# Value products of a head pair as one scheduling unit in two attention stages

## The chip, the cores and the metric

The kernel runs as one program on one core of a Trainium2 chip. The metric is the device time of one launch in microseconds (us), median of the runs shown. Lower is better. Engines are named as the profile names them: PE is TensorE (PEld its weight loads), DVE is VectorE, ACT is ScalarE, POOL is GpSimd, SP is the engine that issues the DMAs here.

## The reference

Two blocks of two layers each follow one another on 512 tokens of width 1024. Layer 0 is a gated pooling mixer, layer 1 stick-breaking attention, layer 2 latent attention (MLA) with a context of 256 tokens, layer 3 differential attention; each is followed by a residual step. The two stages that matter here, cut down:

```python
# stick-breaking attention, 16 heads of 64, strictly causal
A[t,s] = beta[t,s] * prod_{s<j<t} (1 - beta[t,j])      # beta = sigmoid(q.k / sqrt(d))
o = einsum('bhts,bhsd->bhtd', A, v)

# latent attention, 16 heads, values of width 64, 512 tokens and 256 context tokens
p   = softmax(q @ [k, k_c].T * scale);   o   = p @ [v, v_c]
p_c = softmax(q_c @ k_c.T * scale);      o_c = p_c @ v_c
```

## The kernel before

The code is written in Python that records instructions into a tile framework. The framework's scheduler decides in what order each engine's instructions stand: it takes them by readiness and priority in a simulated time, and puts the semaphore waits in. The order of the source is thus a wish, not the order on the engine. Every engine then runs its own list strictly in order.

Both attention stages work by `pipeline`: a list of steps, each with a `first` part (logits on PE, then the elementwise work on ACT, DVE and POOL) and a `second` part, called some steps later, which turns the probabilities (`transpose`, line 172, into a PSUM tile `aT_p` or `PT_p`, then a copy to SBUF). Between the steps stand "pieces": projections that fill PE (`z_p`, `kb_p`, `vb_p`, `qb_p`) and the `ada` products (line 768), whose operands `araw` come by DMA from HBM.

When a pair of heads is finished, the products of probabilities and values are made:

- In the stick-breaking stage (414 to 547 us), once for each of 8 pairs: line 726, 8 matmuls into the PSUM tile `pv` (`pv1` in the source), for 4 key blocks j and the two heads e of the pair. Head 0 writes partitions 0 to 63 and head 1 partitions 64 to 127, so each matmul uses 64 columns of the array (128*64 in the profile).
- In the latent stage (780 to 1057 us), twice for each of 8 pairs: line 1057, 12 matmuls of 512 tokens for `PT` and 4 of 256 context tokens for `PTc`, again 128*64, with the two heads in turn.

A profile shows two MATMUL records for each of these fp32 matmuls, so that "x4" is two matmuls, one of each head, and "x2" a single one. The result is multiplied by the gate on DVE (lines 728 and 1058).

Weights come through `wraw`, three buffers of 512 KB that `araw` shares (lines 116 and 765): SP issues a DMA as soon as a buffer is free, ACT rounds it (line 126), POOL takes the rest (line 127).

Of the kernel before, what the change touches and what calls it, by code (L numbers as in the profile page):

```python
# [19 lines left out]
P = 128  # L20
# [3 lines left out]
NT = S // P  # L24
# [17 lines left out]
class Block:  # L42
# [601 lines left out]
    def stick_steps(self, c, ks, qs, vtok, ogs, pool):  # L644


        nc = self.nc
        h = {}
        half = (slice(0, 64), slice(64, 128))
        f = lambda ap: ap.bitcast(F32)  # L650

        def prep():

            Q = h["Q"] = [pool.tile([P, 512], F32R, tag=f"Q{e}", name="Q1", bufs=2) for e in range(2)]
            QL = h["QL"] = [pool.tile([P, 512], F32R, tag=f"QL{e}", name="QL1", bufs=2) for e in range(2)]
            K = h["K"] = [pool.tile([P, 512], F32R, tag=f"K{e}", name="K1", bufs=2) for e in range(2)]
            cs = slice((c % 2) * P, (c % 2 + 1) * P)
            pr = self.p_tr("kT_p")
            for t in range(NT):
                self.transpose(pr[:, t * P:(t + 1) * P], ks[c // 2][:, t, cs])  # L660
            for e in range(2):
                s, o = half[e], half[1 - e]
                nc.scalar.copy(K[e][s], pr[s])
                nc.vector.tensor_tensor(out=K[e][o], in0=pr[s], in1=f(K[e][s]), op=ALU.subtract)
            pr = self.p_tr("qT_p")
            for t in range(NT):
                self.transpose(pr[:, t * P:(t + 1) * P], qs[c // 2][:, t, cs])
            for e in range(2):
                s, o = half[e], half[1 - e]
                nc.scalar.activation(Q[e][s], pr[s], AF.Copy, scale=self.gqk[s])  # L670
                nc.scalar.activation(Q[e][o], pr[s], AF.Copy, scale=self.gqk[s])
                nc.vector.scalar_tensor_tensor(out=QL[e][s], in0=pr[s], scalar=self.gqk[s], in1=f(Q[e][s]), op0=ALU.mult, op1=ALU.subtract)
                nc.scalar.copy(QL[e][o], f(QL[e][s]))
            h["aT"] = [pool.tile([P, 13, P], F32, tag="aT", name="aT", bufs=4) for e in range(2)]

        def first(n, segs):
            if n == 0 and c == 0:
                prep()
            Q, QL, K = h["Q"], h["QL"], h["K"]
            L = self.p_lg("sb_l")  # L680
            for e, i, o in segs:
                w = (i + 1) * P
                qi = slice(i * P, (i + 1) * P)
                nc.tensor.matmul(L[:, o:o + w], lhsT=Q[e][:, qi], rhs=K[e][:, :w], start=True, stop=False)
                nc.tensor.matmul(L[:, o:o + w], lhsT=QL[e][:, qi], rhs=K[e][:, :w], start=False, stop=False)
                nc.tensor.matmul(L[:, o + i * P:o + w], lhsT=self.identb, rhs=self.maskb, start=False, stop=True)
            kp = pool.tile([P, 1024], F32, tag="sb_k", name="sb_k", bufs=2)
            bt = h["bt", n] = pool.tile([P, 1024], F32, tag="sb_b", name="sb_b", bufs=4)
            vw = (lambda t: t) if len(segs) == 3 else (lambda t: t.rearrange("p (a b) -> p a b", b=512)[:, :, :256])
            nc.scalar.activation(vw(kp), vw(L), AF.Sigmoid, scale=-1.0)  # L690
            nc.scalar.activation(vw(bt), vw(L), AF.Sigmoid)
            for e, i, o in segs:
                w = (i + 1) * P
                rev = slice(o + w - 1, o - 1 if o else None, -1)
                nc.vector.tensor_tensor_scan(out=kp[:, rev], data0=kp[:, rev], data1=kp[:, rev], initial=1.0, op0=ALU.mult, op1=ALU.min)  # L695

            for o, w in ((0, 1024),) if len(segs) == 3 else ((0, 256), (512, 256)):
                nc.gpsimd.tensor_tensor(out=bt[:, o:o + w - 1], in0=bt[:, o:o + w - 1], in1=kp[:, o + 1:o + w], op=ALU.mult)  # L698
            if n == 1 and "next" in h:
                h["next"]()  # L700

        def second(n, segs):
            aT, bt = h["aT"], h["bt", n]
            b0, pr = 0, None
            for e, i, o in segs:
                if b0 + i + 1 > 4:
                    b0, pr = 0, None
                if pr is None:
                    pr = self.p_tr("aT_p")
                for j in range(i + 1):  # L710
                    self.transpose(pr[:, (b0 + j) * P:(b0 + j + 1) * P], bt[:, o + j * P:o + (j + 1) * P])
                src = pr[:, b0 * P:(b0 + i + 1) * P].rearrange("p (j t) -> p j t", t=P)
                if i == 3:
                    nc.scalar.copy(aT[e][:, 3 * i:4 * i + 1, :], src)
                else:
                    nc.vector.tensor_copy(out=aT[e][:, 3 * i:4 * i + 1, :], in_=src)
                b0 += i + 1
            if n < 2:
                return
            self.need(c + 1)  # L720
            pv = self.p_pv("pv1")
            for j in range(NT):
                for e in range(2):
                    hd = 2 * c + e
                    av = aT[e][:, 4 * j:10 + j:3, :]
                    nc.tensor.matmul(pv[64 * e:64 * e + 64, j * P:], lhsT=vtok[j][:, hd * 64:(hd + 1) * 64], rhs=av, start=(j == 0), stop=(j == NT - 1))
            og = ogs[c // 2][:, (c % 2) * 512:(c % 2 + 1) * 512]
            nc.vector.tensor_tensor(out=og, in0=pv, in1=og, op=ALU.mult)

        if self.last_pair is not None:  # L730
            self.last_pair["next"] = prep
        self.last_pair = h
        tiles = [[(0, 3, 0), (0, 2, 512), (0, 0, 896)], [(1, 3, 0), (1, 2, 512), (1, 0, 896)], [(0, 1, 0), (1, 1, 512)]]
        return [(lambda n=n, t=t: first(n, t), lambda n=n, t=t: second(n, t)) for n, t in enumerate(tiles)]


# [261 lines left out]
    def mla_steps(self, h, grp, kTs, og, ogc, pool):  # L998
        nc = self.nc
        g, hh, e = h // 4, h % 4, h % 2  # L1000
        H = {}
# [39 lines left out]
        def second(qb):  # L1041
            for pe, dst, i in H[qb]:
                self.probs_T(pe, dst, i)
            if qb < 4:
                return
            if e == 0:
                return
            c = h // 2
            H0 = H["prev"]
            self.need(8 * g + 1)  # L1050
            V = grp["V", g]
            for nk, n, k0, px, o in ((6, 512, 0, "pt", og[c]), (2, 256, 4, "ptc", ogc[c])):
                pv = self.p_pv("pv2")[:, :n]
                for k in range(nk):
                    for ee, HH in ((0, H0), (1, H)):
                        vs = slice((hh - 1 + ee) * 64, (hh + ee) * 64)
                        nc.tensor.matmul(pv[64 * ee:64 * ee + 64, :], lhsT=V[:, k0 + k, vs], rhs=HH[px][:, k, :], start=(k == 0), stop=(k == nk - 1))  # L1057
                nc.vector.tensor_tensor(out=o, in0=pv, in1=o, op=ALU.mult)

        if self.chain:  # L1060
            self.chain[-1]["next"] = prep
            H["prev"] = self.chain[-1]
        self.chain.append(H)
        return [(lambda q=q: first(q), lambda q=q: second(q)) for q in range(5)]

    def soft(self, L, pool, W, bufs):
# [432 lines left out]
```

## Time and profile before

| what | value |
|---|---|
| median of 3 runs | 1595.64 us (1595.2 to 1601.13) |
| profiled execution, its own time | 1594.69 us |
| span of the profile | 1592.9 us |
| PE busy over the span | 1505.3 us (95%) |
| DVE, ACT, POOL busy | 58%, 46%, 38% |
| granted PE clock over the span, share of full | 0.983 |

The span is the time between the first and the last instruction of the profiled execution; 1.8 us of its time lie around it. A busy PE says that a matmul was in the array, not that it ran at its peak. [...]

### The profile page before, as it was taken

Reading aid. Unit: us, or ns where it says so; the run is one execution under the profiler, and the core shown is the slowest. Engines: PE = TensorE matmul, PEld = TensorE weight load, DVE = VectorE, ACT = ScalarE, POOL = GpSimd, SP = SyncE. Lnnn points to the kernel's source line nnn. Section 1 sums busy time; section 2 is a strip of 40 time slices with the busy share of each in tenths; the row PEclk is TensorE's granted clock in tenths of the full one; section 3 lists DMA queues with packets and bytes.
Section 4 is the critical chain, followed back from the end, with each engine's and each line's share of the span. In section 5 each row is a group of like instructions: output and inputs, shape, how many; then the busy total and the mean of one; then the engine's idle time right before and its main releaser. Section 6 shows DMA issues by size and latency. Waiting matters only on the chain.

```text
span 1592.9 us, 24439 instructions
## 1 busy us (share of the span) xinstructions
PE 1505.3 (95%) x9590; PEld 1253.3 (79%) x9590; DVE 927.9 (58%) x1769; ACT 733.8 (46%) x1347; POOL 603.4 (38%) x431
## 2 busy tenths in 40 slices
PE   6999999999899899999999999999798999999997
PEld 4777889997555678888876657579697999999987
DVE  6676465523766656442465566546866555556576
ACT  5323344436566433332565455543235554555642
POOL 2534555553444453212333222435442324343310
PEclk9999999999999999999999999999898999999999
DMA  5322432223244334311103030425421112111122
GB/s 157 105 79 89 123 118 83 98 84 115 81 132 133 106 120 124 87 44 50 50 1 120 5 120 2 145 80 186 132 69 55 41 41 67 40 56 52 54 74 100
DMA packets 149747, 136.01 MB, mean 85 GB/s; under 512 B 12612, under 2 KB 135224, under 8 KB 149632
## 3 DMA queue, kind: packets, MB, share of 16 engines
q1 hardware_dynamic: 149632, 134.45, 27.3%
q8 instruction: 76, 1.25, 0.3%
q14 instruction: 39, 0.32, 0.1%
HBM read 126.02 MB, written 8.40 MB: 84 GB/s over the span
## 4 chain that ended last, share of the span: by engine, by line
PE 41%; DVE 6%; ACT 5%; issue 3%; DMA 2%; POOL 1%; SPq 0%; DVEq 0%; POOLq 0%; ACTq 0%
PE PT_p L172 5%; PE pv L1057 4%; PE qkv_p L147 2%; PE qkv_p L149 2%; PE qkv_p L148 2%; PE pv L1420 2%; PE gt_p L147 2%; PE gt_p L148 2%; PE gt_p L149 2%; PE lg L147 2%; PE lg L148 2%; PE lg L149 2%; PE ada_p L768 1%; ACT pe L1074 1%; DMA wraw<-in_out_w_dram 1%
## 5 line engine op out<-in xcount | busy, mean ns | idle before, releaser
L127 POOL TENSOR_TENSOR wl<-wraw,wh 128x1024 fp32r<-128x1024 f32 (+2 forms) x159 | 376.4, 2376 | 379.5 <-ACT wh L126 366.3
L126 ACT CAST wh<-wraw 128x1024 fp32r<-128x1024 f32 (+2 forms) x164 | 166.4, 1020 | 281.2 <-issue 57.9
L1074 ACT ACTIVATE pe<-lg,st 128x768 f32<-128x768 f32 x160 | 130.5, 816 | 76.7 <-DVE st L1073 60.6
L1073 DVE TENSOR_REDUCE st<-lg 128x1 f32<-128x768 f32 x160 | 133.9, 845 | 38.4 <-PE lg L1401 20.1
L1036 POOL TENSOR_SCALAR pe<-pe,st 128x768 f32<-128x768 f32 (+1 forms) x96 | 73.6, 767 | 159.2 <-DVE st L1075 154.0
L147 PE MATMUL qkv_p<-wh,h 128*128 128x256 f32 x384 | 109.9, 286 | 0.8 <-ACT V L1346 0.7
L172 PEld LDWEIGHTS PT_p<-ident,pe 128*128 128x128 f32 x640 | 72.3, 142 | 47.8 <-issue 16.5
L149 PE MATMUL qkv_p<-wh,h 128*128 128x256 f32 x384 | 108.6, 283 | 0.2 <-DVE h L217 0.2
L148 PE MATMUL qkv_p<-wl,h 128*128 128x256 f32 x384 | 108.7, 283 | 0.0
L172 PE MATMUL PT_p<-ident,pe 128*128 128x128 f32 x640 | 99.9, 282 | 8.0 <-DVE pe L1406 3.0
L1405 POOL TENSOR_SCALAR pe<-pe,st 128x768 f32<-128x768 f32 x32 | 29.2, 912 | 126.2 <-DVE st L1404 80.3
L147 PE MATMUL out_p<-wh,o 128*128 128x256 f32 x256 | 74.7, 293 | 0.9 <-DVE y L1272 0.8
L147 PEld LDWEIGHTS qkv_p<-wh,h 128*128 128x128 f32 x384 | 73.1, 190 | 3.0 <-ACT V L1346 1.3
L148 PE MATMUL out_p<-wl,o 128*128 128x256 f32 x256 | 74.0, 291 | 1.3 <-POOL wl L127 1.3
L149 PE MATMUL out_p<-wh,o 128*128 128x256 f32 x256 | 73.7, 291 | 0.1
L149 PEld LDWEIGHTS qkv_p<-wh,h 128*128 128x128 f32 x384 | 73.0, 190 | 0.4 <-DVE h L217 0.4
L148 PEld LDWEIGHTS qkv_p<-wl,h 128*128 128x128 f32 x384 | 73.2, 191 | 0.0
L147 PE MATMUL kv_p<-wh,kv 128*128 128x256 f32 x256 | 72.1, 282 | 1.2 <-ACT kv L219 1.2
L148 PE MATMUL kv_p<-wl,kv 128*128 128x256 f32 x256 | 71.6, 280 | 0.0
L149 PE MATMUL kv_p<-wh,kv 128*128 128x256 f32 x256 | 71.1, 280 | 0.0
L698 POOL TENSOR_TENSOR sb_b<-sb_b,sb_k 128x1023 f32<-128x1023 f32 (+1 forms) x32 | 43.0, 1354 | 64.7 <-DVE sb_k L695 36.7
L695 DVE TENSOR_TENSOR_SCAN sb_k<-sb_k 128x512 f32<-128x512 f32 (+3 forms) x64 | 61.7, 1007 | 7.6 <-ACT sb_k L690 7.3
(456 smaller groups left out, 4568.1 us busy)
## 6 DMA issues: line engine op xcount, KB each, us to landing
araw<-in_ada_w_dram SPq DMA_DIRECT2D x48, 512.0 KB
wraw<-in_diff_w_in_dram SPq DMA_DIRECT2D x32, 512.0 KB
wraw<-in_out_w_dram SPq DMA_DIRECT2D x24, 512.0 KB
wraw<-in_a_w_in_dram SPq DMA_DIRECT2D x16, 512.0 KB
wraw<-in_ple_gate_w_dram SPq DMA_DIRECT2D x16, 512.0 KB
wraw<-in_w_kv_dram SPq DMA_DIRECT2D x16, 512.0 KB
wraw<-in_b_w_in_dram SPq DMA_DIRECT2D x16, 512.0 KB
wraw<-in_mla_w_in_dram SPq DMA_DIRECT2D x11, 512.0 KB
```

The costliest lines, as they stand in the source:

```text
L126: nc.scalar.copy(h[:, :n], raw[:, :n])
L127: (nc.vector if i < 3 or pool == "ow3" else nc.gpsimd).tensor_tensor(out=l[:, :n], in0=raw[:, :n], in1=h[:, :n].bitcast(F32), op=ALU.subtract)
L147: mm(out, lhsT=lh, rhs=rh, start=start, stop=False)
L148: mm(out, lhsT=lh, rhs=rl, start=False, stop=False)
L149: mm(out, lhsT=ll, rhs=rh, start=False, stop=stop)
L172: self.nc.tensor.transpose(out, in_, self.ident[:in_.shape[0], :in_.shape[0]])
L695: nc.vector.tensor_tensor_scan(out=kp[:, rev], data0=kp[:, rev], data1=kp[:, rev], initial=1.0, op0=ALU.mult, op1=ALU.min)
L698: nc.gpsimd.tensor_tensor(out=bt[:, o:o + w - 1], in0=bt[:, o:o + w - 1], in1=kp[:, o + 1:o + w], op=ALU.mult)
L1036: nc.gpsimd.tensor_scalar(out=pe, in0=pe, scalar1=st[:, 1:2], scalar2=0.0, op0=ALU.mult, op1=ALU.add)
L1057: nc.tensor.matmul(pv[64 * ee:64 * ee + 64, :], lhsT=V[:, k0 + k, vs], rhs=HH[px][:, k, :], start=(k == 0), stop=(k == nk - 1))
L1073: nc.vector.tensor_reduce(out=st[:, 0:1], in_=L, axis=AX.X, op=ALU.max, negate=True)
L1074: nc.scalar.activation(pe, L, AF.Exp, bias=st[:, 0:1], accum_out=st[:, 2:3])
```

## The change

The value products of a pair are put into a `tile_critical` section: one for each pair of the stick-breaking stage (8) and two for each pair of the latent stage (16), 24 in all. A section is one unit for the scheduler: nothing else is put between its instructions.

```diff
             pv = self.p_pv("pv1")
-            for j in range(NT):
-                for e in range(2):
-                    hd = 2 * c + e
-                    av = aT[e][:, 4 * j:10 + j:3, :]
-                    nc.tensor.matmul(pv[64 * e:64 * e + 64, j * P:], lhsT=vtok[j][:, hd * 64:(hd + 1) * 64], rhs=av, start=(j == 0), stop=(j == NT - 1))
+
+            with self.tc.tile_critical():
+                for j in range(NT):
+                    for e in range(2):
...
                 pv = self.p_pv("pv2")[:, :n]
-                for k in range(nk):
-                    for ee, HH in ((0, H0), (1, H)):
...
+
+                with self.tc.tile_critical():
+                    for k in range(nk):
+                        for ee, HH in ((0, H0), (1, H)):
...
```

The built program shows what a section becomes. Each is a block of instructions of its own on PE; all five engines leave their list by a branch there and go on in the next block. On PE two further instructions stand around it (NO_OP), and the branch into the section holds waits. The lines of the kernel move by 2 below the first section and by 4 below the second: line 726 becomes 728, line 1057 becomes 1061.

First place: PE at the first pair of the latent stage. `pv` is the result of the products, `lg` the logits of a later step, `kb_p` a projection, `PT_p` and `qT_p` turned tiles. Before:

```order
L147 MATMUL lg_7149<-kTs_5790,qT_6924 128x512
L172 MATMUL qT_p<-ident,qs 96x128 x4
L148 MATMUL lg_7149<-kTs_5790,qT_6924 128x512
L172 MATMUL qT_p<-ident,qs 96x128 x2
L1057 MATMUL pv_7129<-PT,V 64x512 x2
L147 MATMUL kb_p<-kvlat,wh 128x256
L148 MATMUL kb_p<-kvlat,wh 128x256
L149 MATMUL kb_p<-kvlat,wl 128x256
L1057 MATMUL pv_7129<-PT,V 64x512 x2
L172 MATMUL PT_p<-ident,pe 128x128 x4
L1057 MATMUL pv_7129<-PT,V 64x512 x7
L149 MATMUL lg_7149<-kTs_5790,qT_6924 128x512
```

One further matmul of this unit stands 69 rows earlier, by itself. In the changed program, with the waits of each row:

```order
L148 MATMUL lg_7169<-kTs_5806,qT_6940 128x512
L172 MATMUL qT_p<-ident,qs 96x128 [waits Activation_49]
L172 MATMUL qT_p<-ident,qs 96x128
L1057 NO_OP [waits PE_sequencer_49,DVE_49,Activation_49]
L149 MATMUL lg_7169<-kTs_5806,qT_6940 128x512
L1499 UNCONDITIONAL_BRANCH [waits DMAHW2_49,DMAHW1_49,DMAHW3_49,DMAHW0_49,DMAHW4_49,PE_sequencer_49,DMAHW5_49,DVE_49,DMAHW6_49,PE_49,DMAHW7_49,Activation_49,Pool_49]
L1061 MATMUL pv_7145<-PT,V 64x512 x12
L1057 UNCONDITIONAL_BRANCH
L147 MATMUL lg_7169<-kTs_5806,qT_6940 128x256 [waits PE_49]
L1057 NO_OP [waits PE_sequencer_49]
L148 MATMUL lg_7169<-kTs_5806,qT_6940 128x256
L149 MATMUL lg_7169<-kTs_5806,qT_6940 128x256
```

The 12 products now stand together, and the branch ahead of them waits for all eight DMA queues, for DVE, ACT and POOL, and for PE itself; the row behind them waits for PE again. The values waited for are those that each engine reaches at the end of its own list ahead of the branch, so that everything listed there has to be finished. The four products of `PTc` stood together before, too, and get a section and a branch of the same kind.

Second place: PE at the third pair of the stick-breaking stage; `ada_t` are four small products of an `ada` piece. Before:

```order
L685 MATMUL sb_l<-K_4059,QL_4057 128x384
L726 MATMUL pv_4099<-aT,vtok_1840 64x512 x2
L726 MATMUL pv_4099<-aT,vtok_1841 64x384 x2
L726 MATMUL pv_4099<-aT,vtok_1842 64x256 x2
L726 MATMUL pv_4099<-aT,vtok_1843 64x128 x2
L775 MATMUL ada_t<-asel,ada_row 128x4 x4
```

Changed:

```order
L685 MATMUL sb_l<-K_4063,QL_4061 128x384
L723 NO_OP [waits PE_sequencer_49,DVE_49,Activation_49]
L777 MATMUL ada_t<-asel,ada_row 128x4 [waits DVE_49,Activation_49]
L777 MATMUL ada_t<-asel,ada_row 128x4 x3
L172 MATMUL aT_p<-ident,sb_b 128x128 [waits PE_49,Pool_49]
L1499 UNCONDITIONAL_BRANCH [waits DMAHW2_49,DMAHW1_49,DMAHW3_49,DMAHW0_49,DMAHW4_49,PE_sequencer_49,DMAHW5_49,DVE_49,DMAHW6_49,PE_49,DMAHW7_49,Activation_49,Pool_49]
L728 MATMUL pv_4103<-aT,vtok_1840 64x512 x2
L728 MATMUL pv_4103<-aT,vtok_1841 64x384 x2
L728 MATMUL pv_4103<-aT,vtok_1842 64x256 x2
L728 MATMUL pv_4103<-aT,vtok_1843 64x128 x2
L723 UNCONDITIONAL_BRANCH
L172 MATMUL aT_p<-ident,sb_b 128x128 [waits PE_49]
```

The products stood together before as well; what is new is the branch and that `ada_t` now stands ahead of it.

Third place: the DMAs that SP issues around the third pair's branch in the changed program (a branch on SP marks the end of the list that PE waits for):

```order
L116 DMA wraw_4169<-in_b_w_in_dram 128x8x128
L767 DMA araw_4204<-in_ada_w_2_dram 128x1024
L767 DMA araw_4208<-in_ada_w_2_dram 128x1024
L116 DMA wraw_4349<-in_b_w_in_dram 128x8x128
L1499 UNCONDITIONAL_BRANCH
L767 DMA araw_4385<-in_ada_w_2_dram 128x1024
```

The weight load `wraw_4349` is the last DMA ahead of the branch; before there was no branch, and no PE instruction waited for it at this place. Outside the two stages the lists of PE are the same in both programs: the first 2276 and the last 3691 of 9112 matmuls and loads.

## Rows read from the trace of the kernel before

**Rows 1.** Stages: window, length; busy us of PE, PEld, DVE, ACT, POOL; clock; DMA.

```profile
414.00:547.00 133.00, 118.91 (x666) 76.31 (x664) 87.66 (x131) 73.49 (x107) 65.11 (x40) 0.96 0.34 107
780.00:1057.00 277.00, 272.74 (x1581) 179.87 (x1580) 168.33 (x412) 157.06 (x356) 92.15 (x114) 0.99 0.19 58
```

**Rows 2.** PE in order of time, first latent pair: start, duration, line.

```profile
787.66 1.07 PE L1057 MATMUL pv<-PT,V 128*64 128x512 f32 x2
...
803.22 1.08 PE L1057 MATMUL pv<-PT,V 128*64 128x512 f32 x4
...
806.38 3.65 PE L1057 MATMUL pv<-PT,V 128*64 128x512 f32 x14
809.95 0.50 PE L149 MATMUL lg<-kTs,qT 96*128 96x512 f32 x1
```

**Rows 3.** PE in order of time: two matmuls in a row of 512 columns.

```profile
790.22 0.40 PE L148 MATMUL lg<-kTs,qT 96*128 96x512 f32 x1
790.45 0.39 PE L149 MATMUL lg<-kTs,qT 96*128 96x512 f32 x1
```

**Rows 4.** All engines in time: a copy on ACT and PE, which waited for it.

```profile
412.00 0.57 ACT L714 COPY aT<-aT_p 128x512 f32<-128x512 f32 x1
...
412.65 0.19 PEld L684 LDWEIGHTS sb_l<-K,Q 128*128 128x128 f32 x1 [0.84 <-ACT aT L714]
412.65 0.50 PE L684 MATMUL sb_l<-K,Q 128*128 128x512 f32 x1
```

**Rows 5.** Start of the program on POOL, across the only branch into the kernel's block.

```profile
0.34 0.10 POOL L1487 MEMSET const-uint8-127<- 128x1 uint8 x1
0.73 0.20 POOL masks.py:197 MEMSET ident<- 128x128 f32 x1 [0.29 <-POOLq L1487]
```

**Rows 6.** The page's DMA queue of instruction loads: packets, MB, share of 16 engines.

```profile
q8 instruction: 76, 1.25, 0.3%
```

**Rows 7.** All engines in time at the first, third, fifth and eighth stick-breaking pair.

```profile
414.52 2.37 PE L726 MATMUL pv<-aT,vtok 128*64 128x512 f32 x16
...
416.88 1.04 ACT L126 CAST wh<-wraw 128x1024 fp32r<-128x1024 f32 x1 [0.53 <-DMA wraw<-in_b_w_in_dram]
...
460.69 2.37 PE L726 MATMUL pv<-aT,vtok 128*64 128x512 f32 x16
...
462.99 1.06 PE L775 MATMUL ada_t<-asel,ada_row 128*128 128x4 f32 x8
...
463.68 1.04 ACT L126 CAST wh<-wraw 128x1024 fp32r<-128x1024 f32 x1 [2.72 <-DMA wraw<-in_b_w_in_dram]
...
500.98 2.38 PE L726 MATMUL pv<-aT,vtok 128*64 128x512 f32 x16
...
504.14 1.04 ACT L126 CAST wh<-wraw 128x1024 fp32r<-128x1024 f32 x1 [2.89 <-DMA wraw<-in_b_w_out_dram]
...
543.68 2.96 PE L726 MATMUL pv<-aT,vtok 128*64 128x512 f32 x16
...
544.16 0.37 SPq L116 DMA_DIRECT2D wraw<-in_b_w_out_dram  x1
```

**Rows 8.** Two stretches of 1 us behind it, columns as in rows 1.

```profile
546.00:547.00 1.00, 1.00 (x7) 0.57 (x4) 0.26 (x1) 1.00 (x4) 0.00 (x0) 1.00 1.00 303
547.00:548.00 1.00, 0.80 (x3) 0.19 (x1) 1.00 (x3) 1.00 (x4) 0.00 (x0) 1.00 0.72 101
```

**Rows 9.** DVE in time at the first latent pair.

```profile
802.89 0.69 DVE L996 TENSOR_TENSOR kTs<-kb_p,kTs 64x512 fp32r<-64x512 f32 x1
```

**Rows 10.** The third latent pair: PE in time, and a stretch of 1 us.

```profile
875.77 1.94 PE L1057 MATMUL pv<-PT,V 128*64 128x512 f32 x8
...
876.00:877.00 1.00, 1.00 (x6) 0.29 (x4) 0.94 (x2) 1.00 (x2) 0.00 (x0) 1.00 0.43 168
```

**Rows 11.** The longest idle time of PE in the stick-breaking stage, and the clock behind it.

```profile
426.49 1.12 PE L172 MATMUL qT_p<-ident,qtok 128*128 128x128 f32 x4 [3.73 <-DVE aT L716]
...
425.00:430.00 5.00, 3.51 (x11) 2.93 (x12) 3.55 (x5) 1.97 (x4) 2.27 (x3) 0.53 0.21 81
```

More of the change, by code (lines that the diff above doesn't have):

```diff
@@ L721, in second @@
             pv = self.p_pv("pv1")
-            for j in range(NT):
-                for e in range(2):
-                    hd = 2 * c + e
-                    av = aT[e][:, 4 * j:10 + j:3, :]
-                    nc.tensor.matmul(pv[64 * e:64 * e + 64, j * P:], lhsT=vtok[j][:, hd * 64:(hd + 1) * 64], rhs=av, start=(j == 0), stop=(j == NT - 1))
+            with self.tc.tile_critical():
+                for j in range(NT):
+                    for e in range(2):
+                        hd = 2 * c + e
+                        av = aT[e][:, 4 * j:10 + j:3, :]
+                        nc.tensor.matmul(pv[64 * e:64 * e + 64, j * P:], lhsT=vtok[j][:, hd * 64:(hd + 1) * 64], rhs=av, start=(j == 0), stop=(j == NT - 1))
             og = ogs[c // 2][:, (c % 2) * 512:(c % 2 + 1) * 512]
@@ L1053, in second @@
                 pv = self.p_pv("pv2")[:, :n]
-                for k in range(nk):
-                    for ee, HH in ((0, H0), (1, H)):
-                        vs = slice((hh - 1 + ee) * 64, (hh + ee) * 64)
-                        nc.tensor.matmul(pv[64 * ee:64 * ee + 64, :], lhsT=V[:, k0 + k, vs], rhs=HH[px][:, k, :], start=(k == 0), stop=(k == nk - 1))
+                with self.tc.tile_critical():
+                    for k in range(nk):
+                        for ee, HH in ((0, H0), (1, H)):
+                            vs = slice((hh - 1 + ee) * 64, (hh + ee) * 64)
+                            nc.tensor.matmul(pv[64 * ee:64 * ee + 64, :], lhsT=V[:, k0 + k, vs], rhs=HH[px][:, k, :], start=(k == 0), stop=(k == nk - 1))
                 nc.vector.tensor_tensor(out=o, in0=pv, in1=o, op=ALU.mult)
```

## The prediction

> **What bounds the kernel now.** I began with the busy time of the engines in the two stages [rows 1]. PE is busy for 272.74 of 277.00 us in the latent stage and 118.91 of 133.00 in the stick-breaking stage; the next engine, DVE, has 168.33 and 87.66. PE is therefore the bound in both: what shortens or delays PE's list shows in the end nearly in full, while the other engines have room, about 100 us and 45 us. The 14.1 us that PE stands idle in the stick-breaking stage are the only place where a new wait of PE might cost nothing.
>
> Next I read PE's rows in order of time around one latent pair, for what the change can gain [rows 2]. The 12 products of `PT` appear as x2 at 787.66 (one matmul by itself, 1.07 us), x4 at 803.22 (1.08 us), and the first seven matmuls of the x14 at 806.38 (3.65 us); another single one lies between the first two. A single matmul thus takes as long as two matmuls, one of each head. The two heads use 64 columns each, and side by side they run at the same time. One step in a chain of such pairs takes 1.94 - 1.08 = 0.86 us [rows 2, 10].
>
> Last I looked, at the pairs themselves, for what else is under way when the products start, since that is what the new branch will wait for [rows 7, 9, 10].
>
> **The gain.** Of a `PT` group of 12, two matmuls now run alone. By rows: 2 x 1.07 for the singles, 1.08 for the x4, and about 3.65 for the last seven, 6.87 in all. Grouped it is five steps of 0.86 and a last one of 1.08, 5.37. The 1.5 us that this gives back are less by two or three overlaps: a matmul that follows another one starts 0.23 us after it but takes 0.40 [rows 3], and most of such an overlap was there with the neighbours already. I take 1.3 us for each pair, 8 x 1.3 = **10.4 us** (10 to 12). The four `PTc` products and at least five of the eight stick-breaking groups stood together before, as the third pair does (2.37 us, x16) [rows 7], so 16 sections can gain nothing or next to nothing; what the other stick-breaking groups may gain I leave in the range.
>
> **The price of a bare section.** Every section empties PE before it and again behind it, since PE waits for itself at both places. I work one such edge out in three parts:
> - the lost overlap: 0.40 us for a matmul less the 0.23 us at which the next would have started, 0.17 [rows 3];
> - the semaphore: ACT's copy ends at 412.00 + 0.57 = 412.57, and the PE weight load that waited for it starts at 412.65, 0.08 [rows 4];
> - the first matmul behind a stop takes 0.50 instead of 0.40, 0.10 [rows 3, 4].
>
> Together 0.35, and two of them 0.70. Then there are two jumps of PE's list. No row shows a jump of PE in the stages. The nearest is at the start of the program, where POOL's MEMSET ends at 0.44 and the next starts at 0.73 behind the branch into the kernel's block, 0.29 [rows 5]; part of that may be the end of a write. The bounds are 0 and 0.29 for each jump. I take 0.10, since a jump to the instruction that stands next in memory has less to do than the start of a program. That makes 0.70 + 0.20 = 0.90 us a section, and 24 x 0.90 = **21.6 us**. The low bound has no cost of a jump and half of each edge (a weight load can run beside the wait): 24 x 0.35 = 8. The high bound is 24 x (0.70 + 0.58) = 31.
>
> **What the branch waits for beyond PE itself.** It waits for everything that stands in any engine's list ahead of it, all eight DMA queues too. In the stick-breaking stage this is mostly a weight load of 512 KB that SP gave out shortly before, and that no PE instruction needed yet:
> - First pair: the products started at 414.52; the DMA that ACT's cast waited for was there at 416.88 [rows 7]. That is 2.36, less about 1.06 us of PE work that now stands ahead, 1.3.
> - Third: 463.68 against 460.69, 3.0, less 0.9, because `ada_t` (462.99, 1.06 us long) and a turned block now stand ahead of the branch and fill PE: 2.1.
> - Fifth: 504.14 against 500.98, 3.2, less the same 0.9: 2.3.
> - Eighth: the load is given out at 544.16 [rows 7]. The DMA engines are full up to 547.00 and at 0.72 in the next microsecond [rows 8], so I put the landing at 547.3, 3.6 us behind the start of the products at 543.68.
>
> The sum is **9.3 us**. If SP gives these loads out so much earlier that they are half done, 3 are left; if the other four pairs meet one as well, it is 17. Queued behind the branch on PE are the products and the logits of the next step, on which ACT and DVE wait; so a wait here is not made up elsewhere.
>
> In the latent stage the DMAs are rarer (share 0.19 against 0.34 [rows 1]). At the third pair DMA is still at 0.43 in the microsecond up to 877.00, and the products started at 875.77: 1.2 [rows 10]. Otherwise the branch waits for DVE or ACT to end what they have in hand. At the first pair DVE's L996 ends at 802.89 + 0.69 = 803.58, and PE could have gone on at 803.22 + 0.23 (the spacing in [rows 3]) = 803.45: 0.13 [rows 2, 9]. 15 times that is 2.0, together **3.2 us**. Low bound 1 (only the third pair); high bound 16, if each section meets a whole further operation of DVE's 0.69 us [rows 9] and the DMAs of the third pair come again.
>
> [...]
>
> **What is absorbed.** PE's idle 14.1 us in the stick-breaking stage come from waits for DVE and ACT. While PE stands at a branch these catch up, so that the wait that follows is shorter. I take **-3** (0 to -8, about half of the idle time), since most of the new waits are for DMAs and lie elsewhere than the old ones.
>
> The branches of the other engines wait for nothing and lie in their free time; were that cover gone, they would cost 48 jumps of 0.10 each, 5 us. The lists of PE outside the two stages are the same, so I cost them at nothing.
>
> **Sum:** 1594.69 - 10.4 + 21.6 + 9.3 + 3.2 + 4 - 3 = 1619.4. The median of the runs is 0.95 above the profiled execution's own time; with that, 1620.
>
> [...]
>
> **The rivals.**
> - *Edges nearly free* (the other side). If the next weight loads and the sequencer's work run while PE empties, and if what the branch waits for is done by the time PE reaches it, a section costs some 0.3 us (one lost overlap of 0.17 and some semaphore). Then it is -10.4 + 24 x 0.3 + 2 = -1, and with a gain of 12 and 0.2 a section, -12 + 5 + 1 = -6: 1590 to 1595, still up to a microsecond lower if a stick-breaking group gains. For it speaks that PE's waits in the profile cost only 0.08 of semaphore; against it, that the DMAs in [rows 7] were not yet there. It decides below 10.4/24 = 0.43 us a section with no DMA waited for.
> - *A load of instructions at each jump.* The instruction queue moved 76 packets in 0.3% of 16 engines' span [rows 6], 0.003 x 16 x 1592.9 / 76 = 1.0 us each. With 48 jumps that is +48 in place of the 4.8: about 1663, and 1669 with the clock lowered more often. Against it: PE runs through 9112 matmuls and loads with no such stop to be seen, and the blocks follow each other.
> - *The engines that feed PE are stopped too.* In the latent stage ACT and DVE work ahead of PE. If PE now waits at all 16 branches for one whole operation of theirs, which PE would have met later at no cost, each costs some 0.69 more [rows 9]: +11, 1631.
> - *The change does nothing.* If the products stand together anyway, as 16 of the groups did, and the barriers fall into idle time, the time stays at 1595. The 4.3 us of idle time in the latent stage [rows 1] leave too little room for 16 sections; I count this with the first rival.
>
> **How the numbers follow.** A measurement of this kernel can tell about 0.5%, 8 us, from no change: 1587.7 to 1603.6 is "the same". The likely case has 0.55; its terms put it between 1600 and 1640. The edges that are nearly free have 0.23, of which a part lies under 1587.7, where stick-breaking gains would have to come on top: 0.08 faster. Stopped feeders have 0.14 and the loads of instructions 0.08. A range of 1598 to 1650 leaves out most of the first rival and the dearest one. Slower by over 0.5%: 0.55 + 0.14 + 0.08, 0.77; the same, 0.15.
>
> **What would show it.** Gain: the `PT` products as one row of x24 of some 5.4 us, no x2 by themselves. Edges: in the latent stage an idle time of PE ahead of each L1061 and behind it, together near 0.9 us; at 0.3 the first rival is right, at 2 the second, with more than a hundred packets in the instruction queue. Loads: at the first, third, fifth and eighth stick-breaking pair an idle time of 1 to 4 us that ends with a DMA. Clock: windows of 5 us behind those with less than 0.9. The prediction is wrong if both stages together grow by less than 8 us, or if the idle time sits elsewhere than at the 24 sections.

## The result

| kernel | median | runs |
|---|---|---|
| before | 1595.42 us (1593.05 to 1601.13) | 4 |
| changed | 1650.95 us (1647.45 to 1655.31) | 4 |

The changed kernel takes 1.0344 times as long (95% interval 1.0306 to 1.0381), 55.5 us more. The sign and the kind of cost were forecast; the size was not: 1620 was forecast, 24 us more, and the time lies just above the range, which ended at 1650.

### The profile page after: what moved, and what is told of

Same layout as the page of the kernel before. It is cut to its first block, busy times and chain, and to the rows that moved or that the text cites. A ratio compares the mean times of both kernels' runs of the same rounds, so it can differ in the third digit from the quotient of the medians.

```text
span 1648.0 us, 24761 instructions
## 1 busy us (share of the span) xinstructions
PE 1506.5 (91%) x9590; PEld 1255.4 (76%) x9590; DVE 919.4 (56%) x1769; ACT 733.3 (44%) x1347; POOL 600.7 (36%) x431
## 5 line engine op out<-in xcount | busy, mean ns | idle before, releaser
L127 POOL TENSOR_TENSOR wl<-wraw,wh 128x1024 fp32r<-128x1024 f32 (+2 forms) x159 | 376.4, 2376 | 394.5 <-ACT wh L126 372.4
L698 POOL TENSOR_TENSOR sb_b<-sb_b,sb_k 128x1023 f32<-128x1023 f32 (+1 forms) x32 | 42.5, 1337 | 84.2 <-DVE sb_k L695 60.9
L695 DVE TENSOR_TENSOR_SCAN sb_k<-sb_k 128x512 f32<-128x512 f32 (+3 forms) x64 | 57.2, 935 | 7.1 <-ACT sb_k L690 6.9
```

The lines of the kernel that those rows point to most:

```text
L127: (nc.vector if i < 3 or pool == "ow3" else nc.gpsimd).tensor_tensor(out=l[:, :n], in0=raw[:, :n], in1=h[:, :n].bitcast(F32), op=ALU.subtract)
```

## The profile after

The stages first, in the view of the stretches (window, length; busy us of PE, PEld, DVE, ACT, POOL; clock; DMA), the stick-breaking stage from the end of the logits ahead of the first pair to the first output product, and most of the latent stage:

```profile
414.92:578.46 163.54, 124.10 (x659) 75.71 (x659) 82.81 (x129) 71.35 (x103) 62.07 (x40) 0.87 0.28 87
815.00:1109.41 294.41, 264.17 (x1564) 177.67 (x1563) 163.20 (x407) 150.79 (x341) 90.97 (x113) 0.98 0.18 55
```

The same stretch of the stick-breaking stage was 132.05 us before, with 117.95 of PE busy (414.52 to 546.57). It is 31.5 longer: PE's idle time went from 14.1 to 39.4 us, +25.3, and its busy time rose by 6.2 at a granted clock of 0.87 of full speed against 0.96. Most of the loss is thus standing still; the slower products come on top.

To compare kernels I use the same four PE instructions in each trace: the start of the last `ada_p` ahead of the first pair (411.66 before, 411.99 changed), the first `o_p` (546.57, 578.46), the first `lat_ss` (698.30, 732.55) and the first `out_p` (1056.18, 1109.41):

| us | stick-breaking | between | latent |
|---|---|---|---|
| before | 134.9 | 151.7 | 357.9 |
| changed | 166.5 (+31.6) | 154.1 (+2.4) | 376.9 (+19.0) |

The rest, ahead of these and behind them, adds 2.2 to the span. In the runs below the programs are the same ahead of the first of these points, and yet the traces take 411.7 to 418.5 us to it. So a cost is read inside a stage, and a whole kernel by its median.

PE in order of time, the products of the eight stick-breaking pairs, with the idle time ahead of each in brackets and what ended it (for the first, third, fifth and eighth pair the rows of before are in [rows 7]):

```profile
418.93 3.72 PE L728 MATMUL pv<-aT,vtok 128*64 128x512 f32 x16 [2.92 <-DMA araw<-in_ada_w_dram]
438.33 4.54 PE L728 MATMUL pv<-aT,vtok 128*64 128x512 f32 x16 [4.42 <-DMA araw<-in_ada_w_dram]
471.74 4.53 PE L728 MATMUL pv<-aT,vtok 128*64 128x512 f32 x16 [2.56 <-POOL wl L127]
488.54 2.38 PE L728 MATMUL pv<-aT,vtok 128*64 128x512 f32 x16 [0.96 <-ACT QL L673]
518.26 4.06 PE L728 MATMUL pv<-aT,vtok 128*64 128x512 f32 x16 [2.32 <-DMA gates<-ada_row]
536.18 2.37 PE L728 MATMUL pv<-aT,vtok 128*64 128x512 f32 x16 [0.93 <-ACT QL L673]
554.71 4.54 PE L728 MATMUL pv<-aT,vtok 128*64 128x512 f32 x16 [6.77 <-issue]
573.70 3.90 PE L728 MATMUL pv<-aT,vtok 128*64 128x512 f32 x16 [5.34 <-DMA wraw<-in_b_w_out_dram]
```

The brackets add up to 26.2 us. Behind six of the eight waits the same 16 records take 3.7 to 4.5 us instead of 2.37; the granted clock in these six stretches is 0.50 to 0.62, and 1.00 in the other two.

What the profile names in a bracket is inferred from semaphores, and for the third, fifth and seventh row it misses the load. The built program tells which DMA stands last on SP's list ahead of each branch. SP's rows tell when it was given out, and the trace's semaphore updates when it had landed:

| pair | last DMA ahead of the branch | given out | landed | products start | wait |
|---|---|---|---|---|---|
| 1 | `araw` | 413.54 | 418.56 | 418.93 | 2.92 |
| 2 | `araw` | 433.77 | 437.48 | 438.33 | 4.42 |
| 3 | `wraw` | 466.91 | 471.00 | 471.74 | 2.56 |
| 4 | `araw` | 470.97 | 474.71 | 488.54 | 0.96 |
| 5 | `wraw` | 512.84 | 517.24 | 518.26 | 2.32 |
| 6 | `wraw` | 527.30 | 531.17 | 536.18 | 0.93 |
| 7 | `wraw` | 549.80 | 553.87 | 554.71 | 6.77 |
| 8 | `wraw` | 568.76 | 572.82 | 573.70 | 5.34 |

So each of the six long waits ends 0.4 to 1.0 us behind the landing of a load, and at the two short ones the last load had landed long before. The DMA of the gates named at the fifth pair stands behind the branch on SP's list. POOL, named at the third, ended at 470.94, 0.06 ahead of the landing.

The seventh row names only "issue" as what ended the wait. All engines at that place show what happened before:

```profile
546.52 3.25 POOL L127 TENSOR_TENSOR wl<-wraw,wh 128x1024 fp32r<-128x1024 f32 x1
...
549.80 0.37 SPq L116 DMA_DIRECT2D wraw<-in_b_w_out_dram  x1
551.08 1.99 POOL L698 TENSOR_TENSOR sb_b<-sb_b,sb_k 128x1023 f32<-128x1023 f32 x1 [1.30 <-DVE sb_k L695]
```

POOL ends its work on a weight tile at 549.77; that frees a buffer, and SP gives out the next load at 549.80. DVE is done at 550.90 and POOL at 553.07; PE begins at 554.71, 4.9 us behind the issue. The load's data moves in only part of that (stretches of 1 us, the last two columns are DMA share and GB/s):

```profile
550.00:551.00 1.00, 0.00 (x0) 0.00 (x0) 0.91 (x2) 0.00 (x0) 0.00 (x0) 0.50 0.08 23
551.00:552.00 1.00, 0.00 (x0) 0.00 (x0) 0.00 (x0) 0.00 (x0) 0.93 (x1) 0.50 0.77 222
552.00:553.00 1.00, 0.00 (x0) 0.00 (x0) 0.00 (x0) 0.00 (x0) 1.00 (x1) 0.50 0.81 243
553.00:554.00 1.00, 0.00 (x0) 0.00 (x0) 0.00 (x0) 0.00 (x0) 0.07 (x1) 0.50 0.12 36
```

At the second pair the load has the same story, and the trace of before shows what changed. There POOL ended a second weight tile (L127) at 423.36, ahead of three other steps (L698), and SP gave out the load 10 us before the products (433.12):

```profile
417.89 5.47 POOL L127 TENSOR_TENSOR wl<-wraw,wh 128x1024 fp32r<-128x1024 f32 x2
423.33 3.95 POOL L698 TENSOR_TENSOR sb_b<-sb_b,sb_k 128x1023 f32<-128x1023 f32 x3
423.39 0.33 SPq L765 DMA_DIRECT2D araw<-in_ada_w_dram  x1
```

In the changed kernel that tile stands behind the steps, and the load goes out when PE has reached the branch (433.91):

```profile
429.96 1.43 POOL L698 TENSOR_TENSOR sb_b<-sb_b,sb_k 128x255 f32<-128x255 f32 x2 [0.72 <-DVE sb_k L695]
431.36 2.38 POOL L127 TENSOR_TENSOR wl<-wraw,wh 128x1024 fp32r<-128x1024 f32 x1
433.77 0.33 SPq L767 DMA_DIRECT2D araw<-in_ada_w_dram  x1
```

The latent stage, second to eighth pair in part; x24 is the 12 products of `PT`, x8 the four of `PTc`:

```profile
872.32 5.37 PE L1061 MATMUL pv<-PT,V 128*64 128x512 f32 x24 [0.50 <-ACT qT L1015]
877.78 0.49 PE L149 MATMUL lg<-kTs,qT 96*128 96x512 f32 x1
...
882.75 1.08 PE L1061 MATMUL pv<-PTc,V 128*64 128x256 f32 x8 [0.69 <-ACT pe L1078]
...
915.15 6.84 PE L1061 MATMUL pv<-PT,V 128*64 128x512 f32 x24 [3.61 <-POOL pe L1038]
...
1070.59 7.07 PE L1061 MATMUL pv<-PT,V 128*64 128x512 f32 x24 [2.48 <-DMA wraw<-in_out_w_dram]
...
1107.42 1.08 PE L1061 MATMUL pv<-PTc,V 128*64 128x256 f32 x8 [1.88 <-PEq L1057]
```

The products are one row of 5.37 us, as the prediction worked out from [rows 2, 10]. Where nothing late is waited for, PE idles 0.50 us ahead and 877.78 - 877.69 = 0.09 behind. At the third pair (915.15) the branch waits for a whole chain of the softmax that PE itself had started just before, with logits that ended at 910.18: maximum on DVE, exponential on ACT, reciprocal on DVE, scaling on POOL, which ends at 914.33, 0.82 ahead of the products:

```profile
909.90 0.28 PE L149 MATMUL lg<-kTs,qT 96*128 96x256 f32 x1
...
910.80 0.94 DVE L1077 TENSOR_REDUCE st<-lg 128x1 f32<-128x768 f32 x1
...
912.01 0.89 ACT L1078 ACTIVATE pe<-lg,st 128x768 f32<-128x768 f32 x1
913.10 0.15 DVE L1079 RECIPROCAL st<-st 128x1 f32<-128x1 f32 x1
913.42 0.91 POOL L1038 TENSOR_SCALAR pe<-pe,st 128x768 f32<-128x768 f32 x1 [2.47 <-DVE st L1079]
```

The page's instruction queue, which had 76 packets before [rows 6]:

```profile
q8 instruction: 77, 1.26, 0.3%
```

## The experiments

Theory A: a section costs what its branch waits for, mostly loads given out shortly before. Theory B: each section costs the same. Theory C: the grouping itself costs. Ratios are to the kernel before.

**One part at a time.** The diff is the change's own, kept for line 728 alone, for `PT` alone, or for `PTc` alone:

```diff
-                with self.tc.tile_critical():
+                with (self.tc.tile_critical() if px == "pt" else contextlib.nullcontext()):
```

> The eight sections of the stick-breaking stage alone, the latent stage as before. Theory A (a section makes PE wait for everything given out before it, DMAs and the work behind them above all): in the trace of the changed kernel the stick-breaking stage grew by 31.5 us (163.54 against 132.05), of which 25 us are idle time of PE, so this kernel comes out near 1595.4 + 31.5 = 1627, with about 26 us of idle time ahead of the products. Theory B (the price is the same for every section, as my sum had it): 8 of 24 sections take a third of the 55.5, +18, 1614.

> Sections around the 12 products of PT alone (8), those of PTc and the stick-breaking stage as before. Theory A: eight bare sections at about 1.0 us, two long waits (3.6 and 2.5 us, less 0.5 each) of 5 us, 3 us of lower clock behind these, less the gain of 10.4: +6, 1601. Theory B: the gain of 10.4 stays what it is and each section costs 55.5 + 10.4 over 24, 2.7 us: +12, 1607. If grouping gains nothing at all: +16, 1611.

> Sections around the 4 products of PTc alone (8), which stood together before, so there is nothing to gain and the price of a section in the latent stage shows by itself. Theory A: 8 x 1.0 and one or two us of waits, +10, 1605. Theory B: 8 x 2.7 = +22, 1617. My prediction's 0.9 and 0.13 for a section: +8, 1603.

| sections kept | median | ratio | stick-breaking | latent |
|---|---|---|---|---|
| stick-breaking | 1630.06 us | 1.0212 (1.0185 to 1.0240) | +28.8 | +0.1 |
| `PT` | 1607.23 us | 1.0071 (1.0049 to 1.0092) | +0.1 | +10.5 |
| `PTc` | 1607.10 us | 1.0082 (1.0050 to 1.0114) | -0.6 | +8.7 |

The parts add up (28.8 + 10.5 + 8.7 = 48.0 of the 50.6 in the two stages), and eight sections in one stage cost 28.8, in the other 8.7: theory B is wrong for the stick-breaking stage. The median of the first run is 34.3 above that of before, more than the 28.8 in the stage; 1.9 more lie between the stages, and the rest where the programs are the same. `PTc` has nothing to gain and nothing late but the work in hand, so 8.7 / 8 = 1.1 us is the price of a section with ordinary company; by PE's idle time in the stage (4.2 before, 14.4 here, at a clock of 1.00 against 0.99) it is 1.3. `PT` came out at theory B's 1607, not at A's 1601: 10.5 / 8 = 1.3 us for each section even net of what the grouping gives back.

**The stage without loads.** With and without sections, the weights of that stage read from one buffer (their values left out):

```diff
-            u["raw"] = self.wp.tile([P, 1024], F32, tag="wraw", name="wraw", bufs=3)
-            for dst, src in u["src"](self._w_view(u["raw"], u["shape"])):
+            u["raw"] = self.keep if self.no_loads else self.wp.tile([P, 1024], F32, tag="wraw", name="wraw", bufs=3)
+            for dst, src in () if self.no_loads else u["src"](self._w_view(u["raw"], u["shape"])):
```

`araw` was treated alike.

> The eight stick-breaking sections as in the run with those alone, but in this stage no weights are loaded: the projections and the ada products there read one buffer that was loaded once, so their values are left out. To be set against the same kernel without sections. Theory A (the branch waits for loads that were given out shortly before it): of the 25.3 us of idle time ahead of the products some 20 end with a load; they go, and what is left is 8 edges of 1.0, waits for ACT and POOL of 0.5 to 1 each and the gates' DMA of 1.8: this kernel is 12 to 16 us longer than the one without sections. Theory B (a price for each section whatever is under way): still 34 longer.

> No section; in the stick-breaking stage no weights are loaded, as in the run beside it (values left out there). PE is the bound there and seldom waits for a load, so near 1595; the loads of the next stage's first weights are gone too, at most 3 us either way.

Measured: 1610.11 us (1.0074, 1.0049 to 1.0099) with sections and 1595.16 us (0.9987, 0.9974 to 0.9999) without, 15 apart instead of 34 (the two traces are 11 apart); in the stage 144.2 against 134.0, 10.2 instead of 28.8. That is inside theory A's 12 to 16 for the time. What PE still waits for ahead of the products, the four largest groups (columns: us in total, times, longest; three more are of 0.4 to 0.6 us):

```profile
PE pv L733 <- DMA wraw<-in_b_w_out_dram: 4.9, 1, 4.9
PE pv L733 <- POOL sb_b L703: 3.6, 2, 3.0
PE pv L733 <- POOL wl L128: 1.8, 1, 1.8
PE pv L733 <- ACT QL L678: 0.9, 1, 0.9
```

The third and the fifth pair wait 0.44 and 0.57 here, so their waits went with the loads, whatever the brackets named. The largest one left is the eighth pair's load; weights for the next stage are loaded again from 521.95 on. So the loads of the stage, with what follows from their waits, are 18.6 of the 28.8 us, and the one at the end is half of what remains.

**More work for PE during the wait.** The same eight products stand once more ahead of each section:

```diff
+            for j in range(NT):
+                for e in range(2):
+                    ...
+                    nc.tensor.matmul(pv[64 * e:64 * e + 64, j * P:], lhsT=vtok[j][:, hd * 64:(hd + 1) * 64], rhs=av, start=(j == 0), stop=(j == NT - 1))
             with self.tc.tile_critical():
```

> The eight stick-breaking sections, and ahead of each the same eight products once more outside the section (into the same tile, overwritten by the section's), so that PE has 2.4 us more to do while the branch waits. It tells the clock from the wait. If the time is a wait for loads and other engines, the added work lies inside it at the pairs that waited 2.5 us or more and costs about 1.5 us at each of the two that waited 0.9, and a little at the fifth: +4 without a clock. If the lower clock behind the waits costs what the trace suggests (the eight groups took 30.5 us in place of 19 at full speed), a busier PE gets 6 to 10 of this back: 1624 to 1628, faster with more work. Without any clock effect 1634; if the waits aren't for others but for PE's own jumps, all of 19: 1649.

Measured: 1643.13 us (1.0272, 1.0245 to 1.0300), 13 above the run with the sections alone; the stage is 180.1, 16.4 longer, for some 20 us of added products. The expectation missed, and the rows say why:

```profile
429.30 4.43 PE L733 MATMUL pv<-aT,vtok 128*64 128x512 f32 x16 [7.18 <-issue]
...
480.71 4.32 PE L733 MATMUL pv<-aT,vtok 128*64 128x512 f32 x16 [3.95 <-DMA araw<-in_ada_w_dram]
```

The waits didn't get shorter (23.9 us in all against 25.3); they moved: the first is 7.18 in place of 2.5, the second 0.63 in place of 4.2, the sixth 4.42 in place of 0.9. The scheduler, which counts in its own time, found room for one more load ahead of the first branch. SP's list there (the number of the row first), with the sections alone and with the added work:

```
57 L767 DMA araw<-in_ada_w_dram 128x1024 x2
58 L116 DMA wraw<-in_b_w_in_dram 128x8x128
59 L767 DMA araw<-in_ada_w_dram 128x1024
60 L1497 UNCONDITIONAL_BRANCH
```

```
58 L116 DMA wraw<-in_b_w_in_dram 128x8x128
59 L772 DMA araw<-in_ada_w_dram 128x1024 x2
60 L1502 UNCONDITIONAL_BRANCH
```

The second `araw` is given out at 424.88, when PE has already stood still since 422.12. A later branch thus met a newer load at the first pair; the other pairs I didn't follow one by one. The groups inside the sections took 26.8 us against 28.8, so a better clock gave little back; this run can't price the clock, since the waits moved as well.

**The grouping without a section.** First by the order of the source alone, then with an order on PE's list:

```diff
-                for k in range(nk):
-                    for ee, HH in ((0, H0), (1, H)):
+                for k in reversed(range(nk)):
+                    for ee, HH in ((1, H), (0, H0)):
```

The flags that mark the first and the last product follow the new order, and the four products of `PTc` are turned too.

> No section anywhere; the latent products are written from the last key block to the first and with the second head first, so that the first product needs the probabilities that come last and none can be put far ahead by itself. The built program then has pairs only, in two to four pieces of a unit. If the gain of the grouping is real and PE the bound: each pair loses two single matmuls and has about three pieces, 1.08 + 0.86 x 3 in place of 6.87, some 1.0 us for each pair: -8, 1587. If the products' time is hidden anyway or the singles filled holes: 1595.

> The kernel with the latent products reversed and no sections, once more beside the one above on the same chip: 0.9961 of the kernel before, as it was.

> No section; the order on PE that the sections of PT gave, nearly: the products begin with the block that comes last (so that none runs ahead by itself), and whatever the code issues later is put behind the last product of PT by an order on PE's own list, with no semaphore. Eight of 12 products then stand together behind a piece of four. Theory A (the waits of the section cost, not the grouping): the gain is there, 1.0 to 1.2 us for each pair, 1586 to 1588. Theory C (the grouping itself costs, since the products no longer fill PE while it waits for the copies of turned blocks, 7.3 us of such waits in the run with sections of PT against 3.1 before): the gain is eaten by 4 or more, 1592 to 1597.

Reversed: 1589.91 us, 0.9961 (0.9946 to 0.9976), and when taken again 1593.55 us, 0.9977 (0.9968 to 0.9987); the latent stage is 7.3 and 5.9 shorter. For the grouped kernel the key blocks are taken in the order 3, 2, 1, 0, 5, 4, and every later step is put behind the last product of `PT`:

```diff
+            with self.tc.issue_after(self.last_pv.ins) if self.last_pv else nullcontext():
                 if n < len(steps):
                     steps[n][0]()
...
```

It gave 1592.11 us, 0.9966 (0.9952 to 0.9980), with a latent stage 6.1 shorter. There PE waits 7.3 us in the stage against 3.8 before (sum of its waits), so theory C holds for some 3.5 us: products that stand together no longer fill PE while a block is copied. A grouping without a barrier gains all the same.

The gain in the stage has to be read with the clock. The latent stage of the kernel without loads has the code of before, and took 355.4 us at a granted clock of 1.00 where before took 357.9 at 0.99. The reversed (350.6) and the grouped kernel (351.8) ran at 1.00 too, so 4.8 and 3.6 us are the products' part, and the other 2.5 the clock's. PE's busy time fell by 7.0 (350.97 to 343.99, reversed), and its waits took back 2.1.

**Pairs in both stages, no section.** The same turn of the two heads in the stick-breaking products, on top of the reversed latent ones:

```diff
-                for e in range(2):
+                for e in (1, 0):
                     hd = 2 * c + e
```

> No section; the latent products reversed as before, and in the stick-breaking stage the second head of each pair written first, so that no product of the first head runs by itself at the sixth and seventh pair (x2 of 1.07 us alone in the kernel before). If PE's time is what counts there too: 1.0 us less at each of the two, 2 less than with the latent stage alone, which was 5.8 below the kernel before: 1588. If PE's idle time in that stage takes it up (the seventh pair waits 3 us for a copy anyway): no less than with the latent stage alone, 1590.

Measured: 1585.70 us, 0.9935 (0.9920 to 0.9950), faster than both kernels and than the expectation. The stick-breaking stage is 127.7, 7.2 shorter than before, and 4.5 shorter than in the second trace of the reversed kernel, which has that stage as it was, at the same clock of 0.99 (132.2). Its sixth and seventh pair, which ran in two pieces before:

```profile
517.38 2.38 PE L726 MATMUL pv<-aT,vtok 128*64 128x512 f32 x16
...
531.70 2.38 PE L726 MATMUL pv<-aT,vtok 128*64 128x512 f32 x16 [2.38 <-DVE aT L716]
```

All eight now take 2.37 or 2.38, 19 in place of 24.8 us. Before, single products stretched five of them, and a lowered clock the seventh; without that clock, in the second trace of the reversed kernel, the eight took 23.1. So the pairs give 4.1 us here and the clock the rest.

## Why the prediction was wrong

By stage, the sum had 17.5 us for the stick-breaking sections (with waits, clock and what is absorbed), 7.2 for the latent ones and nothing elsewhere; 31.6, 19.0 and 4.6 came. Both stages missed.

**What bounds the kernel**: right. PE's list was the bound in both stages; the waits and products that were added to it made the stages longer.

**The gain of 10.4**: real but too large. The `PT` groups run in 5.37 us as worked out, and PE's busy time in the latent stage fell by 7.4 us (353.69 to 346.33). The kernels that get the pairs without a section gain 3.6 to 4.8 us in the stage at an equal clock; in the grouped one 3.5 us of the gain went into waits for copies that the scattered products had covered. The 6.87 of the first pair was right by luck: what I took for a second single product is a pair (804.78, 1.08 us), and the second single one is in the x14. The sum also put nothing on the stick-breaking groups, of which only three took 2.37 before; there the pairs are worth 4.1.

**The price of a bare section, 0.90 us**: nearly right. The trace has 0.50 of idle time ahead, 0.09 behind, 0.09 for the slower first matmul behind the section (0.49 at 877.78 against 0.40 [rows 3]), and the two overlaps of 0.17, an estimate from [rows 3], that idle time doesn't show: 1.0. What of the 0.50 is the emptying of PE, the semaphores or the jump no row tells. The sections of `PTc` cost 1.1 to 1.3 with what they wait for.

**The jump**: the rival with a load of instructions at each jump is out. The instruction queue moved 77 packets in place of 76, with 48 jumps more on PE alone. The 0.10 us for a jump was my estimate; no run shows a jump by itself.

**What the branch waits for, 9.3 us in the stick-breaking stage**: this is the step that failed. The waits ahead of the products are 26.2 us, or 22.2 without the 0.50 of each bare section, above the bound of 17. The four pairs for which I had named a load waited 11.1 of that in place of 9.3, the eighth above all. The other four, at nothing in the sum, waited 11.1 as well, nearly all of it at pairs two and seven (3.9 and 6.3).

I had taken the times of loads and products from the trace of before and asked how late the one was for the other. That can't find the second pair: there its load landed at 426.91, 6 us ahead of the products. The change moved the load itself. It goes out when a buffer comes free, that hangs on POOL's list, and POOL's list was put in another order; so at pairs two and seven the last load ahead of the branch was given out when PE was already there or had 0.1 us to go. The kernel without loads (10.2 in place of 28.8 us) shows that the loads are the cause; the kernel with added work shows that the scheduler decides which load stands ahead of a branch. Why it put POOL's list in another order I didn't trace. A load then takes 4.9 us from its issue to PE's start, not the 3.1 that I had from 544.16 to 547.3 [rows 7, 8]: in the trace of before that load lands at 548.23, and in the changed kernel 0.4 to 1.0 us pass from a landing to PE's start.

**What was absorbed, 3 us**: the size was met, but elsewhere than meant. Of the 14.1 us of before, 3.0 lay ahead of the products themselves (the seventh pair waited for a copy), and the new wait of 6.77 took their place. PE's other idle time did not shrink: 39.4 - 26.2 = 13.2 us against 11.1. The longest of these waits, 3.73 [rows 11], is gone, but others grew by more.

**The clock, 4 us**: too small, which the total hides. No run shows this term by itself; what the runs show in its place is the time of the products. PE's busy time in the stage rose by 6.2 us, near the 4 and the 2.7 of lost overlaps that I had. But the eight groups alone took 30.0 us where they take 19.0 at full speed (2.37 or 2.38 each at a granted clock of 1.00). That is 11.0 by the lower clock, against 1.7 before, 9.3 more; the 4.1 us that the pairs gained went against it. So about 9 us of the 31.6 are the clock's, read from rows of one trace; no run changed the clock alone.

**The latent waits, 3.2 us**: too small. PE's idle time in the stage rose by 26.3 us (4.2 to 30.5), against 14.4 + 3.2 in my sum. Ahead of the 16 groups it is 16.3 us, 8.3 more than 0.50 for each; elsewhere in the stage it is 14.2 against 3.4, waits for copies mostly, which the sum had at nothing. Two waits ahead of products (3.61 for a chain of the softmax, 2.48 for a load, in the kernel with `PT` alone 3.25 and 3.19) and the lower clock behind them, 6.84 and 7.07 for 5.37, are 8 us. The rival of the stopped feeders, +11, comes nearer to this cost than my main case did.

The 2.4 us between the stages stay open: 1.6 of them are one longer wait ahead of `lat_p` (2.7 us against 1.1), but why it is longer I didn't trace. They come with the stick-breaking sections (1.9 with those alone, 2.4 without loads, none with the added work).

## What to carry to other kernels

Here a barrier cost what was newest in any list ahead of it: six waits of 2.3 to 6.8 us ended 0.4 to 1.0 us behind the landing of the last load. So ask of every engine and of the DMA issuer what the last entry before the barrier is, when it can start and how long it takes from there, rather than how late last run's transfers were. When a buffer comes free, and so which load is new, can change with the barrier itself. If all that is wanted is an order on one engine, get it from the order of the source or an order on that engine alone: turning the loops so that the last operand comes first gave the pairs in both stages and 0.65% instead of a loss of 3.4%.

## What the hardware showed

A load of 512 KB with the DMA engines otherwise empty (share 0.00 from 546 to 550) was given out at 549.80. By the trace's packet records its data moved from 550.85 to 553.48; it had landed at 553.87, 4.1 us behind the issue, and PE began another 0.8 us later. The load of the eighth pair took 4.1 and 0.9.

The lower clock follows many of the waits, but not each wait of the same length. In the trace of before the clock behind the wait of 3.03 us that ends at 531.05 is 0.50 up to 534.5; behind one of 3.58 us that ends at 1150.60 it is 1.00. In the two traces of the reversed kernel, one and the same program, the seventh stick-breaking pair waits 3.04 and 3.05 us; the 14 records behind it took 4.53 us at a granted clock of 0.50 in the first, and 2.37 us at 1.00 in the second.
